# Running sums through memory, substitution in turns, and other places for weights in a three-block network kernel

## The chip, the cores and the metric

The kernel runs on one core of one Trainium2 chip. The metric is the device time of one execution in microseconds (us). The kernel before takes 1947.57 us, the median of three runs (1945.8 to 1948.2).

## The reference

The input x has 256 tokens of 1024 channels, in fp32 throughout. A first block runs two layers, each of four sublayers with an RMS norm before and after: an FFN (1024 to 2816 to 1024, SiLU-gated, half residual), a mixer, a cross attention to a memory of 256 tokens, and another FFN. A second block of one layer follows (a state-space branch beside dilated attention, then an FFN of the same sizes) and a last norm.

The mixer is where most of the change lies. It has retention heads beside four gated delta-rule heads of 128 channels, the latter in both directions over the sequence in chunks of 64. What bears on the change:

```python
g = jnp.cumsum(g.reshape(b, h, n, c), axis=-1)
decay = jnp.exp(jnp.where(tril, g[..., :, None] - g[..., None, :], -jnp.inf))
lower = jnp.where(strict, jnp.einsum('bhnid,bhnjd->bhnij', k_beta, k) * decay, 0.0)
sol = lax.linalg.triangular_solve(lower, rhs, left_side=True, lower=True, unit_diagonal=True)
```

## The kernel before

**Weight products.** Every product with a weight is three fp32r matmuls (`mm3`, L168 to L172), since a weight is kept as a high part `hi` and a rest `lo`: hi·hi, hi·lo, lo·hi. A unit of weights (128 x 1024) comes by DMA from SP's queue into a `raw` tile (L143), ACT makes `hi` from it (L148), DVE `lo` (L149). In the trace L170, L171 and L172 are therefore nearly all of PE's matmuls. There are two ways to multiply: with the activations stationary and 512 columns of weights moving ("by tokens", and DN), or with the weights stationary and 256 columns of activations moving ("by channels").

**Pools.** A pool that isn't named otherwise is opened on the left side of SBUF and stacked upward; in the map of this program `raw` (4 buffers of 4 KB a partition) ends at 42 KB, `wts` (4 `hi`, 4 `lo`) lies at 42 to 75 KB, `xT` at 73 to 108 KB with what follows it, and `hT` of the FFNs (the hidden activations as `hh` and `hl`) at 125 to 154 KB. The pool `w2` (8 `hi`, 8 `lo`), opened on the right side by `more_weights`, lies at 160 to 229 KB.

**Order.** A list scheduler fixes the order on each engine: it takes instructions by their order in the program, but when the next one of an engine isn't ready it takes a later one that is. So PE is filled with later matmuls wherever their inputs stand ready. `issue_after` puts an instruction behind another one.

**An FFN** (L312) goes over 11 slices j of 256 hidden channels. Slices 0 and 1 are made by tokens, since the input's second half comes late (`by_tokens`, with the Tanh of L364, DVE's L365 and L366, and PE's transposes of L371); 2 to 10 by channels (`by_channels`, twice 48 matmuls each). DN(t, j) (L408) multiplies slice j with its rows of the down weights for token half t: 12 matmuls of 512 columns, four products of three. `wpool` (L329) says from which pool a unit's `hi` and `lo` come: for slice 1, and for the down weights of slices 0 and 7 to 10, `w2`; for slice 10's gate and up `wts`; of the others every third call gets `wts`, which is one of the four gate/up units and the first of the two down units of a slice. After the loop the program's order is DN(0,8), DN(0,9), DN(0,10), fin(0), DN(1,7) to DN(1,10), and fin(1), put off to the next stage. `fin(t)` is the norm chain of token half t: squares of the two accumulators on ACT (L205), the inverse root on POOL (L189 to L213), the residual on DVE (L298, L300), and the next norm the same way again, until DVE writes `xg` (L237) and PE transposes it (L250).

With `defer`, the next stage's first norm factor is applied later: `set_pre` (L254) writes xg (L235) without the factor and then queues the squares for the factor. In `ffn` the second half's `fin` runs as `run_late` behind by_tokens(0, 0) in the program (L436 to L438).

**The mixer** (L724). `strengths` (L752) is a generator whose steps are hung into the stream of projections at q steps, by the dictionaries at L958. Its third step makes the sums `ngl` (L764), its fourth and fifth call `decays(0)` and `decays(1)` (L795). For a direction, `decays` makes the running sum of g at all partitions: per token half, four fp32 matmuls with one column of g, repeated over 128 columns, stationary against the triangle `tri` (L805), and a matmul that adds the mask from `identr` and `mskr` (L807). Three such groups (near, far, and the columns 256:384) go through 12 Exps on ACT (L812, L815, L818) from PSUM to E, which `pairs` and `products` (L992, L1000; PE at L1003) use.

**The substitution** `solve` (L1117) solves the chunks of 64 in both directions. Each step makes eight 64-row matmuls (as 64*64 tiles) with M (L1145) and with the diagonal inverses (L1153), over four heads and two directions; the directions lie on opposite halves of the partitions. The program emits both directions in turn, but the scheduler is free to take one direction's first.

## Time and profile before

| | |
|---|---|
| median of three runs | 1947.57 us (1945.8 to 1948.2) |
| the profiled execution | 1947.42 us |
| its span, first to last instruction | 1945.2 us |
| granted TensorE clock, mean | 0.998 of full speed |
| HBM read | 333.90 MB, 172 GB/s over the span |

The span is what the page's shares refer to; the profiled execution's own time is 2.2 us longer, for what lies around it. Times in a timeline are microseconds from the start of the span. A matmul's recorded time is longer than the step from its start to the next one's, since they are pipelined; the steps are what add up. An fp32 matmul appears as two records, an fp32r one as one.

### The profile page before, as it was taken

What the parts mean: (1) busy time and instruction counts of PE and PEld (TensorE: products, weight loads), DVE (VectorE), ACT (ScalarE), POOL (GpSimd) and SP (SyncE); (2) the same over time, 40 slices, a digit from 0 to 9 for tenths busy, and PEclk for the clock granted to TensorE, in tenths of its full rate; (3) what the DMA queues carried; (4) which work ended last, traced back from release to release, by engine and by line L of the source; (5) the groups of instructions that cost most, each with busy time, mean ns of one, the idle gap of its engine ahead of it and who ended that gap; (6) DMA issues with size and microseconds to landing.
All of it is one profiled execution on the core that took longest, in us unless ns stands there. A gap on an engine that the chain in (4) does not pass through costs nothing.

```text
span 1945.2 us, 34675 instructions
## 1 busy us (share of the span) xinstructions
PE 1914.7 (98%) x12859; PEld 1717.7 (88%) x12859; DVE 1412.7 (73%) x3002; ACT 1048.9 (54%) x2173; POOL 185.7 (10%) x407
## 2 busy tenths in 40 slices
PE   9999999999999999999999999999999999999998
PEld 6899888898899989999788978998999998888997
DVE  6777688775666766667987757666798988767765
ACT  5655465465554555546555645554555555546542
POOL 2000100020200110010100120002101111001000
PEclk9999999999999999999999999999999999999999
DMA  8666434364566556644434726655566646656651
GB/s 266 206 220 217 125 109 147 109 220 137 164 205 196 180 186 220 187 161 144 137 101 145 247 86 212 200 189 157 146 174 182 187 121 205 200 196 224 199 179 49
DMA packets 272887, 337.26 MB, mean 173 GB/s; under 512 B 19740, under 2 KB 223150, under 8 KB 272718
## 3 DMA queue, kind: packets, MB, share of 16 engines
q1 hardware_dynamic: 266980, 326.64, 53.6%
q10 hardware_dynamic: 5690, 8.25, 1.2%
q8 instruction: 101, 1.65, 0.3%
q14 instruction: 68, 0.56, 0.1%
q0 software_dynamic: 48, 0.16, 0.0%
HBM read 333.90 MB, written 1.08 MB: 172 GB/s over the span
## 4 chain that ended last, share of the span: by engine, by line
PE 84%; DVE 4%; POOL 3%; DMA 2%; ACT 2%; issue 2%; SPq 0%; ACTq 0%; POOLq 0%; DVEq 0%
PE bank L170 25%; PE bank L171 25%; PE bank L172 25%; DVE lo L149 2%; DMA raw<-in_ffn_up_dram 2%; PE bank L250 1%; POOL t L192 1%; POOL vh L213 1%; POOL y L193 1%; ACT hi L148 1%; PE bank L1003 1%; PE bank L1543 1%; ACT md L1034 1%; PE bank L1153 1%; PE bank L1256 1%
## 5 line engine op out<-in xcount | busy, mean ns | idle before, releaser
L148 ACT ACTIVATE hi<-raw 128x512 fp32r<-128x512 f32 (+1 forms) x1190 | 678.7, 615 | 413.6 <-PE bank L172 96.0
L149 DVE TENSOR_TENSOR lo<-raw,hi 128x512 fp32r<-128x512 f32 (+1 forms) x1190 | 764.7, 680 | 187.1 <-ACT hi L148 178.4
L170 PE MATMUL bank<-xh,hi 128*128 128x256 f32 x2080 | 588.8, 283 | 0.0
L171 PE MATMUL bank<-xl,hi 128*128 128x256 f32 x2080 | 585.1, 281 | 0.0
L172 PE MATMUL bank<-xh,lo 128*128 128x256 f32 x2080 | 584.7, 281 | 0.1
L170 PEld LDWEIGHTS bank<-xh,hi 128*128 128x128 f32 x2080 | 394.2, 190 | 4.1
L171 PEld LDWEIGHTS bank<-xl,hi 128*128 128x128 f32 x2080 | 393.9, 189 | 3.5
L172 PEld LDWEIGHTS bank<-xh,lo 128*128 128x128 f32 x2080 | 394.5, 190 | 0.6 <-DVE lo L149 0.6
L170 PE MATMUL bank<-hi,xh 128*128 128x512 f32 (+1 forms) x852 | 333.5, 392 | 3.5 <-ACT xh L175 2.2
L171 PE MATMUL bank<-lo,xh 128*128 128x512 f32 (+1 forms) x852 | 324.7, 381 | 5.2 <-DVE lo L149 5.1
L172 PE MATMUL bank<-hi,xl 128*128 128x512 f32 (+1 forms) x852 | 323.9, 380 | 0.5 <-DVE xl L177 0.5
L171 PEld LDWEIGHTS bank<-lo,xh 128*128 128x128 f32 x852 | 160.3, 188 | 34.8 <-DVE lo L149 9.9
L170 PEld LDWEIGHTS bank<-hi,xh 128*128 128x128 f32 x852 | 160.2, 188 | 31.5 <-ACT xh L175 3.5
L172 PEld LDWEIGHTS bank<-hi,xl 128*128 128x128 f32 x852 | 159.9, 188 | 28.8 <-DVE xl L177 2.2
L170 PE MATMUL bank<-hi,hh 128*128 128x512 f32 x440 | 175.9, 400 | 1.3 <-ACT hh L175 1.3
L171 PE MATMUL bank<-lo,hh 128*128 128x512 f32 x440 | 173.9, 395 | 0.0
L172 PE MATMUL bank<-hi,hl 128*128 128x512 f32 x440 | 173.4, 394 | 0.0
L213 POOL TENSOR_SCALAR vh<-ss 128x1 f32<-128x1 f32 x40 | 27.6, 689 | 1130.8 <-ACT junk L205 996.1
L402 ACT ACTIVATE th<-s 128x256 f32<-128x256 f32 x90 | 37.3, 414 | 124.3 <-DVE s L401 122.7
L172 PEld LDWEIGHTS bank<-hi,hl 128*128 128x128 f32 x440 | 82.7, 188 | 20.7 <-DVE hl L177 0.3
L170 PEld LDWEIGHTS bank<-hi,hh 128*128 128x128 f32 x440 | 82.7, 188 | 18.4 <-ACT hh L175 1.7
L171 PEld LDWEIGHTS bank<-lo,hh 128*128 128x128 f32 x440 | 82.7, 188 | 16.0
(369 smaller groups left out, 1991.4 us busy)
## 6 DMA issues: line engine op xcount, KB each, us to landing
raw<-in_w_in_dram SPq DMA_DIRECT2D x112, 512.0 KB, 4.4
raw<-in_ffn_gate_dram SPq DMA_DIRECT2D x176, 256.0 KB, 3.9
raw<-in_ffn_up_dram SPq DMA_DIRECT2D x176, 256.0 KB, 4.3
raw<-in_ffn_down_dram SPq DMA_DIRECT2D x88, 512.0 KB, 4.6
raw<-in_w_in_dram SPq DMA_DIRECT2D x96, 192.0 KB, 2.8
raw<-in_w_ffn_gate_dram SPq DMA_DIRECT2D x44, 256.0 KB, 3.8
raw<-in_w_ffn_up_dram SPq DMA_DIRECT2D x44, 256.0 KB, 4.1
raw<-in_w_ffn_down_dram SPq DMA_DIRECT2D x22, 512.0 KB, 4.6
```

Of the source, the lines that this page charges most:

```text
L148: nc.scalar.activation(hi[:, c], raw[:, c], AF.Copy)
L149: nc.vector.tensor_tensor(lo[:, c], raw[:, c], hi[:, c].bitcast(F32), ALU.subtract)
L170: mm(out, lhsT=lh, rhs=rh, start=start, stop=False)
L171: mm(out, lhsT=lh, rhs=rl, start=False, stop=False)
L172: mm(out, lhsT=ll, rhs=rh, start=False, stop=stop)
L192: V.tensor_scalar(t, y, y, vh, ALU.mult, ALU.mult)
L193: V.tensor_scalar(y, t, -1.5, y, ALU.add, ALU.mult)
L213: V.tensor_scalar(vh, s[:, 0:1], s[:, 1:2], 0.5 * EPS, ALU.add, ALU.add)
L250: self.nc.tensor.transpose(b[:, i * P:(i + 1) * P], src[:, (q + i) * P:(q + i + 1) * P], self.ident)
L402: last["A"] = nc.scalar.activation(th, s[:, 0], AF.Tanh)
L1003: T.matmul(b[:, j * 256:(j + 1) * 256], lhsT=lhs[:, h, j * P:(j + 1) * P], rhs=rhs[:, h], start=True, stop=True)
L1034: A.activation(md[r, :, :, :, s], mn[r, :, :, c0:c0 + 16].rearrange("p n h a -> p a h n"), AF.Copy, scale=self.half[s][r])
```

## The change

It has four parts.

1. Decays: per layer, four matmuls with the four columns of g stationary give the running sums of both directions and token halves on four partitions; ACT copies them to SBUF, a DMA on GpSimd's queue writes them to memory, and two others read them back to all 128 partitions, 512 KB each. GpSimd adds the mask (`msk`, fp32, in place of `mskr`; `identr` goes), and the Exps read SBUF, the far group first, before the mask is added to its half. The steps of `strengths` are hung at other q.
2. `solve` chains its matmuls so that the directions alternate on PE.
3. `wpool` puts the down weights of slices 2 to 7 into `wts` and all gate and up weights but slice 10's into `w2`; the pool `raw` moves to the right side, so that what lies above it on the left comes 16 KB lower.
4. In an FFN's `run_late`, the squares of the deferred norm are put behind the Tanh of by_tokens(0, 0).

```diff
@@ -73,7 +73,7 @@
         nc = self.nc
         pool = self.pool
         self.cp = pool(ctx, "const", 1)
-        self.rawp = pool(ctx, "raw", 4)
+        self.rawp = ctx.enter_context(tc.tile_pool(name="raw", bufs=4, side="right", reuse_waits="tile"))
         self.wp = pool(ctx, "wts", 4)
         self.xp = pool(ctx, "xT", 2)
         self.nrm = pool(ctx, "nrm", 1)
@@ -98,6 +98,8 @@
 
         self.fence = []
 
+        self.behind = []
+
     def first_block(self, ctx):
 
         self.fp = self.pool(ctx, "first", 1)
@@ -105,8 +107,7 @@
         self.tri.append(self.one(C_TB, P))
         self.half = [self.one(C_HALF + i, 1) for i in range(2)]
         self.odd = [self.one(C_HALF + 2 + i, 1) for i in range(2)]
-        self.identr = self.fp.tile([P, P], F32R, name="identr")
-        self.mskr = [self.fp.tile([P, P], F32R, name=f"mskr{d}") for d in range(2)]
+        self.msk = [self.fp.tile([P, P], F32, name=f"msk{d}") for d in range(2)]
         self.lnret = self.fp.tile([P, 16], F32, name="lnret")[:, 0:1]
         self.nc.gpsimd.memset(self.lnret, -0.5 * math.log(128.0))
 
@@ -258,7 +259,10 @@
         r = None if defer else self.rstd(self.halves(self.x[t]), D, pool)
         xg = self.normed(self.x[t], g, r)
         if defer:
-            r = self.rstd(self.halves(self.x[t]), D, pool)
+            with ExitStack() as es:
+                for ins in self.behind:
+                    es.enter_context(self.tc.issue_after(ins))
+                r = self.rstd(self.halves(self.x[t]), D, pool)
             rh, r2 = self.small(1, "rh"), self.small(1, "r2")
             pool.tensor_scalar(rh, r, 0.5, None, ALU.mult)
             self.mark = pool.tensor_scalar(r2, rh, r, None, ALU.mult)
@@ -321,17 +325,15 @@
             hT = {}
             acc = {}
             pend = []
-            cnt = [0]
             last = {}
             factor = self.factor
             rows = []
 
             def wpool(kind, j):
 
-                cnt[0] += 1
-                if j == 1 or kind == "dn" and (j > 6 or j == 0):
-                    return w2
-                return self.wp if j == 10 or cnt[0] % 3 == 0 else w2
+                if kind == "dn":
+                    return self.wp if 1 < j < 8 else w2
+                return self.wp if j == 10 else w2
 
             def load_gu(j):
                 return [[u.rearrange("p (k a f) -> p k a f", k=2, a=2) for u in self.gate_up(wg, wu, j, q, wpool("gu", j))] for q in range(4)]
@@ -434,7 +436,9 @@
             xT = self.xT
             by_tokens(0, 0)
             done = [last["A"].ins, last["V"].ins]
+            self.behind = done[:1]
             self.run_late()
+            self.behind = []
             by_tokens(0, 1, {4: flush, 6: lambda: self.take_pre(1)})
             self.fence = done
 
@@ -646,9 +650,8 @@
         nc.scalar.dma_start(self.cst1, self.a["consts"][:, C_ONE:C_END])
         once = self.nrm.tile([P, C_ALL - C_END], F32, tag="xg", name="once", bufs=2)
         nc.scalar.dma_start(once, self.a["consts"][:, C_END:])
-        nc.scalar.copy(self.identr, self.ident)
         for d, c0 in enumerate((C_MF, C_MB)):
-            nc.scalar.copy(self.mskr[d], once[:, c0 - C_END:c0 - C_END + P])
+            nc.scalar.copy(self.msk[d], once[:, c0 - C_END:c0 - C_END + P])
         self.cs1 = []
         for t in range(2):
             wk = self.nrm.tile([P, 512], F32, tag="junk", name="wk")
@@ -727,6 +730,7 @@
         w_in = a["w_in"][l]
         with ExitStack() as es:
             bp = self.pool(es, "mix", 1)
+            dp = es.enter_context(self.tc.tile_pool(name="drows", bufs=1, space=bass.MemoryType.DRAM))
             wk = self.pool(es, "mixw", 6)
             ch4 = lambda: bp.tile([P, 1024], F32, tag="ch4", name="ch4", bufs=8)
             xg4 = lambda: self.nrm.tile([P, D], F32, tag="xg", name="xg4", bufs=2)
@@ -763,6 +767,17 @@
                     for d in range(2):
                         T.matmul(pg[:, t * 8 + d * 4:t * 8 + d * 4 + 4], lhsT=self.tri[d], rhs=g[:, t, d * 4:d * 4 + 4], start=True, stop=True)
                 V.tensor_scalar(ngl, pg[:, 0:16].rearrange("p (t c) -> p t c", t=2), -1.0, None, ALU.mult)
+
+                b, r = self.bank(), w512()
+                for d in range(2):
+                    for t in range(2):
+                        T.matmul(b[0:4, (2 * d + t) * P:(2 * d + t + 1) * P], lhsT=g[:, t, d * 4:d * 4 + 4], rhs=self.tri[d], start=True, stop=True)
+                A.copy(r[0:4], b[0:4])
+                rows_d = dp.tile([2, 2, 4, P], F32, name="rows_d")
+                nc.gpsimd.dma_start(rows_d.rearrange("d t h c -> h (d t) c"), r[0:4].rearrange("h (x c) -> h x c", c=P))
+                for d in range(2):
+                    rows.append(ch4())
+                    nc.gpsimd.dma_start(rows[d], rows_d[d].rearrange("t h c -> (t h c)").unsqueeze(0).to_broadcast([P, D]))
                 yield
                 decays(0)
                 yield
@@ -790,7 +805,7 @@
             def values(n, hooks={}, between=None):
                 return (self.proj_tokens(mT, a["xattn_v"][l], n * 512, put_v(n), between=between), 4, hooks)
 
-            E, ngc = [None, None], S("ngc", 8)
+            E, ngc, rows = [None, None], S("ngc", 8), []
 
             def decays(d):
                 E[d] = bp.tile([P, 4, 384], F32, tag=f"E{d}", name="E")
@@ -799,23 +814,17 @@
                 c = slice(d * 4, d * 4 + 4)
                 near, far = (slice(0, P), slice(P, 2 * P)) if d == 0 else (slice(P, 2 * P), slice(0, P))
 
-                def rows(t, masked):
-                    b = self.bank()
-                    for h in range(4):
-                        T.matmul(b[:, h * P:(h + 1) * P], lhsT=g[:, t, d * 4 + h:d * 4 + h + 1].to_broadcast([P, P]), rhs=self.tri[d], start=h == 0, stop=h == 3 and not masked)
-                    if masked:
-                        T.matmul(hd(b), lhsT=self.identr, rhs=self.mskr[d].unsqueeze(1).to_broadcast([P, 4, P]), start=False, stop=True)
-                    return hd(b)
-                b = rows(f, True)
-                V.tensor_tensor(ngc[:, c], b[:, :, end], ngl[:, f, c], ALU.add)
+                R = rows.pop(0).rearrange("p (t h c) -> p t h c", t=2, h=4)
+                mask = self.msk[d].unsqueeze(1).to_broadcast([P, 4, P])
+                V.tensor_tensor(ngc[:, c], R[:, f, :, end], ngl[:, f, c], ALU.add)
+                nc.gpsimd.tensor_tensor(R[:, f], R[:, f], mask, ALU.add)
                 for h in range(4):
-                    A.activation(E[d][:, h, near], b[:, h], AF.Exp, bias=ngl[:, f, d * 4 + h:d * 4 + h + 1])
-                b = rows(s, False)
+                    A.activation(E[d][:, h, far], R[:, s, h], AF.Exp, bias=ngc[:, d * 4 + h:d * 4 + h + 1])
+                nc.gpsimd.tensor_tensor(R[:, s], R[:, s], mask, ALU.add)
                 for h in range(4):
-                    A.activation(E[d][:, h, far], b[:, h], AF.Exp, bias=ngc[:, d * 4 + h:d * 4 + h + 1])
-                b = rows(s, True)
+                    A.activation(E[d][:, h, near], R[:, f, h], AF.Exp, bias=ngl[:, f, d * 4 + h:d * 4 + h + 1])
                 for h in range(4):
-                    A.activation(E[d][:, h, 256:384], b[:, h], AF.Exp, bias=ngl[:, s, d * 4 + h:d * 4 + h + 1])
+                    A.activation(E[d][:, h, 256:384], R[:, s, h], AF.Exp, bias=ngl[:, s, d * 4 + h:d * 4 + h + 1])
 
             def sums(x, tag):
 
@@ -955,7 +964,7 @@
             side = strengths()
             s = lambda: next(side, None)
             fill = self.stream([
-                values(0, between=lambda: self.take_pre(1)), *qkv(1, {0: s}), *qkv(2, {0: s, 1: s, 3: s}),
+                values(0, between=lambda: self.take_pre(1)), *qkv(1, {0: s, 3: s}), *qkv(2, {2: s, 3: s}),
                 tokens(512, "rk", {3: lambda: turn("rk")}),
                 tokens(1024, "rv", {2: lambda: backs["rk"](), 3: take_rv}),
                 tokens(0, "rq", {3: lambda: turn("rq")}),
@@ -1120,6 +1129,8 @@
                 halves = (slice(0, 64), slice(64, P))
                 order = (halves, halves[::-1])
                 Z = [inv[d].rearrange("p (h n) i -> p h n i", h=4) for d in range(2)]
+                turns = [(h, d) for h in range(4) for d in range(2)]
+                in_turn = lambda one: self.tc.issue_after(one.ins) if one else nullcontext()
                 for n in range(2):
                     y = [hd(Y[d][:, seq[d][n]]) for d in range(2)]
                     rhs = [hd(R[:, seq[d][n]]) for d in range(2)]
@@ -1139,18 +1150,20 @@
                         if m:
 
                             bs = [self.bank() for _ in range(2)]
-                            for h in range(4):
-                                for d in range(2):
-                                    o = order[d][0]
-                                    T.matmul(bs[d][r[d], h * P:(h + 1) * P], lhsT=M[d][o, h, cols[d] + r[d].start:cols[d] + r[d].stop], rhs=y[d][o, h], start=True, stop=True)
+                            one = None
+                            for h, d in turns:
+                                o = order[d][0]
+                                with in_turn(one):
+                                    one = T.matmul(bs[d][r[d], h * P:(h + 1) * P], lhsT=M[d][o, h, cols[d] + r[d].start:cols[d] + r[d].stop], rhs=y[d][o, h], start=True, stop=True)
                             for d in range(2):
                                 V.tensor_tensor(y[d][r[d]], hd(bs[d])[r[d]], rhs[d][r[d]], ALU.add)
                                 rhs[d] = y[d]
                             yield
                         bs = [self.bank() for _ in range(2)]
-                        for h in range(4):
-                            for d in range(2):
-                                T.matmul(bs[d][r[d], h * P:(h + 1) * P], lhsT=Z[d][r[d], h, n], rhs=rhs[d][r[d], h], start=True, stop=True)
+                        one = None
+                        for h, d in turns:
+                            with in_turn(one):
+                                one = T.matmul(bs[d][r[d], h * P:(h + 1) * P], lhsT=Z[d][r[d], h, n], rhs=rhs[d][r[d], h], start=True, stop=True)
                         A.copy(y[0][r[0]], hd(bs[0])[r[0]])
                         V.tensor_copy(y[1][r[1]], hd(bs[1])[r[1]])
                         yield
```

## Rows read from the trace of the kernel before

**Rows 1.** the page's first part: busy time and share of each engine.

```profile
PE 1914.7 (98%) x12859; PEld 1717.7 (88%) x12859; DVE 1412.7 (73%) x3002; ACT 1048.9 (54%) x2173; POOL 185.7 (10%) x407
```

**Rows 2.** the waits of PE: total us, times, longest us.

```profile
PE bank L371 <- DVE h L366: 4.7, 3, 1.7
...
PE bank L250 <- DVE xg L237: 2.7, 3, 1.3
```

**Rows 3.** PE's timeline, the first decays and E's first use: start, us, line, operation.

```profile
238.40 1.05 PE L805 MATMUL bank<-cst,g 128*128 128x128 f32 x8
...
239.21 0.47 PE L807 MATMUL bank<-mskr,identr 128*128 128x512 f32 x1
...
241.53 0.28 PE L170 MATMUL bank<-xh,hi 128*128 128x256 f32 x1
...
260.45 1.89 PE L1003 MATMUL bank<-ch 128*128 128x256 f32 x8
```

**Rows 4.** a window of the first mixer: PE, PEld, DVE, ACT, POOL busy, clock, DMA.

```profile
262.00:266.00 4.00, 4.00 (x19) 3.35 (x18) 4.00 (x20) 0.85 (x2) 0.00 (x0) 1.00 0.44 131
```

**Rows 5.** lines L213, L1526, L812 (ns min/median/max); POOL and DVE timelines at 673.

```profile
L213 POOL TENSOR_SCALAR vh<-ss x40: 286/301/4797, 5.6 to 1750.5; 128x1 f32<-128x1 f32 x40
...
673.95 4.80 POOL L213 TENSOR_SCALAR vh<-ss 128x1 f32<-128x1 f32 x1 [2.83 <-ACT junk L205]
...
673.68 4.90 DVE L149 TENSOR_TENSOR lo<-raw,hi 128x512 fp32r<-128x512 f32 x8
...
L1526 POOL TENSOR_TENSOR w<-xs,dsk x8: 1042/1288/1360, 1403.1 to 1608.9; 128x512 f32<-128x512 f32 x8
...
L812 ACT ACTIVATE E<-bank,ngl x16: 360/369/388, 240.6 to 916.3; 128x128 f32<-128x128 f32 x16
```

**Rows 6.** DMA issues: count, KB each, median us to landing.

```profile
rows<-rows_d SPq DMA_DIRECT2D x8, 512.0 KB, 4.9
...
rows_d<-w SPq DMA_DIRECT2D x1, 32.0 KB, 1.5
```

**Rows 7.** PE's timeline, substitution: both directions, then one alone.

```profile
332.38 1.09 PE L1153 MATMUL bank<-ch,iv 64*64 64x128 f32 x16
...
338.69 1.08 PE L1145 MATMUL bank<-ch,M 64*64 64x128 f32 x8
```

**Rows 8.** PE's timeline: first and last starts of runs of weight products.

```profile
104.09 0.28 PE L170 MATMUL bank<-xh,hi 128*128 128x256 f32 x1
...
109.76 0.40 PE L170 MATMUL bank<-hi,hh 128*128 128x512 f32 x1
...
173.75 0.28 PE L171 MATMUL bank<-xl,hi 128*128 128x256 f32 x1
...
185.15 0.39 PE L170 MATMUL bank<-hi,hh 128*128 128x512 f32 x1
...
204.74 0.39 PE L170 MATMUL bank<-hi,xh 128*128 128x512 f32 x1
...
250.42 0.39 PE L170 MATMUL bank<-hi,xh 128*128 128x512 f32 x1
...
255.65 0.39 PE L172 MATMUL bank<-hi,xl 128*128 128x512 f32 x1
```

**Rows 9.** timelines at FFN ends: ACT and DVE 186:205, PE at the second block.

```profile
192.34 0.60 ACT L205 ACTIVATE junk<-bank 128x512 f32<-128x512 f32 x1 [3.48 <-PE bank L172]
...
203.08 1.42 DVE L237 SCALAR_TENSOR_TENSOR xg<-x,y,gain 128x512 f32<-128x512 f32 x2 [4.04 <-POOL y L193]
...
1359.08 1.10 PE L250 MATMUL bank<-cst,xg 128*128 128x128 f32 x6 [1.31 <-DVE xg L237]
```

**Rows 10.** timelines of ACT and DVE at the start of an FFN.

```profile
496.79 0.45 ACT L364 ACTIVATE th<-bank,rh 128x256 f32<-128x256 f32 x1
...
495.89 1.29 DVE L235 TENSOR_TENSOR xg<-x,gain 128x512 f32<-128x512 f32 x2
...
497.28 0.42 DVE L365 SCALAR_TENSOR_TENSOR th<-th,bank 128x256 f32<-128x256 f32 x1
```

More of the change, by code (lines that the diff above doesn't have):

```diff
@@ L1 @@
 import math
-from contextlib import ExitStack
+from contextlib import ExitStack, nullcontext
 import numpy as np
```

## The prediction

> **What bounds the kernel.** The profile page comes first: PE is busy 1914.7 us, 98% of the span of 1945.2, no other engine over 73% [rows 1]. The waits of PE come second: no cause reaches 6 us, and the two that this change can touch make 4.7 and 2.7 us [rows 2]. So the time is the length of PE's stream of matmuls, and a change is worth what it takes out of that stream or what new holes it opens in it. Third is the timeline of PE around each edit, where start-to-start steps are read, not durations: matmuls overlap, and a 512-column one recorded with 0.39 us starts only about 0.23 us after its forerunner [rows 8]. Last, the other engines' windows in the mixer: DVE is full there in stretches (4.00 of 4 us from 262 to 266 [rows 4], the same in the window before it and from 282 to 302), so what PE gains in the mixer need not all reach the end.
>
> The profiled execution took 1947.42 us (span 1945.2), the median is 1947.57; the sum is made against 1947.4. A measurement tells some 0.2% (3.9 us) from no change.
>
> **Part 1, running sums by way of memory.** One decays call holds PE from 238.40 to 241.53, 3.13 us [rows 3]; it runs for two directions and two layers: 4 × 3.13 = 12.5 us leave PE. Added per layer: four two-pass matmuls of 128 columns, as the four at 238.40 to 239.21, 0.81 us [rows 3], so 1.8 us for two layers with the change of tile. PE: −10.7 us.
> What else is added per layer: an ACT copy of 4x512 (under 0.6 us on an engine that has room before 258 us), a 32 KB write and two 512 KB broadcast reads on POOL's queue, and four 128x512 POOL adds. The nearest rows: such a read landed after 4.9 us from SP's queue [rows 6], such an add took 1.04 to 1.36 us [rows 5]. The new matmuls stand where the strengths step makes its sums now, one q, some 4 us, ahead of 238.40 [rows 3]; from there 2 us for matmuls and copy (estimate), write 1.5, read 4.9 [rows 6], two adds 2.6, twelve Exps 4.4 (12 × 369 ns [rows 5]): the first direction is complete near 250, the second near 253, while the first use of E comes after the products at 260.45 [rows 3]. That leaves 7 us, so the path itself should cost nothing. The Exps stay as many; the PSUM banks that they held are freed.
> Not all 10.7 us arrive. After 258 us DVE is full for stretch upon stretch [rows 4]; and POOL and DVE hold each other up: at 673.95 a 128x1 POOL instruction that takes 301 ns by the median of its line lasted 4.80 us, the time of a DVE row of eight subtractions, 673.68 to 678.58 [rows 5]. Four adds of 1.3 us per layer can so take up to 5 us from DVE. Bounds: −10.7 and 0. I take about half, −5.7: DVE has slack before 258 us and none behind.
> The Trainium skill, "SBUF — State Buffer", section "🔬 SBUF: two separate sides", speaks against this part: a DVE instruction with two SBUF inputs and a GpSimd one that reads SBUF exclude each other for their whole length, and a GpSimd-queue DMA can starve for descriptors while DVE holds the port. By it the adds would cost DVE the full 5 us a layer and the gain would be near nothing. The long POOL row agrees with the first half; no run here shows the second.
> The reordered Exps and the copies of the mask cost nothing: the same count, under other work.
>
> **Part 2, substitution in turns.** A group of both directions together (x16) lasts 1.09 us; one direction alone (x8) lasts 1.08 us [rows 7]. So two directions in turn are as cheap as one: 64-row tiles of opposite halves run side by side. Three of six groups per layer stand split in the trace (338.69 and its partner at 342.20; 344.27 and 345.71; 354.60 and 356.04), six in all; pairing each saves up to 1.08 us on PE. The first matmul may go alone where one direction's input is later. Take −5.5, bounds −2 and −7. What waits for the later direction has other matmuls as filler.
>
> **Part 3, where weights and activations lie.** PE's step depends on where its operands lie. By the program's map the raw pool ends at 42 KB of a partition, wts lies at 42 to 75, xT at 73 to 108, hT at 125 to 154, w2 at 160 to 229. Out of wts with xh (both low) 23 steps of 512 columns take 250.42 to 255.65, 227 ns each; in the tail, out of w2 with hh (both high), 84 take 185.15 to 204.74, 233 ns [rows 8]. A kernel-wide mean over such steps would lie nearer 228.4 and 233.5 (estimate), 5 ns apart. Channel products go the other way, with weights stationary: slice j=10, all out of wts, takes 120.0 ns (95 steps, 173.75 to 185.15), a slice with three of four units in w2 118.1 ns (48, 104.09 to 109.76), so w2 alone 117.5 [rows 8].
> The change puts gate and up of j=2 to 9 wholly into w2: one unit in four, 8 × 24 × 5 FFNs = 960 steps × 2.5 ns = −2.4 us. It puts down slices 2 to 7 (6 × 24 × 5 = 720 steps, now half or wholly from w2) into wts, and with raw moved away hT sinks by 16 KB into the low part: 720 × 4.9 ns = −3.5 us; only −1.6 if hT does not matter. One unit of j=0 goes high: 60 steps × 6 ns, +0.4. Sum −5.0 with a discount, bounds −2.5 and −6.
>
> **Part 4, the tail of an FFN.** Slice 7 of down now sits in wts, of four buffers, which slice 10 of gate and up needs whole. Its last two units can be converted only when DN(1,7) is done, which stood behind fin(0). So DN(0,8), DN(0,9), DN(1,7) and perhaps DN(1,8) go ahead of the second half of by_channels(0,10). PE loses nothing there, but fin(0)'s chain (squares at 192.34, xg to 203.08 + 1.42 = 204.50: 12.2 us [rows 9]) was covered by four DNs, 48 × 0.233 = 11.2 us; one to two and a half (2.8 to 6.8 us) remain, I take two, so 5.6 us of cover go. At the two mixer ends the memory's values fill (0.6 each); at the deferred end, whose chain is shorter, 1.1; at the second block, where PE already waits at 1359.08 [rows 9], 3.5 with less left to wait for later; at the very end 0.5. Sum +6, bounds 0 and +12.
>
> **Part 5, squares behind the first Tanh.** The Tanh starts at 496.79, when the squares are through; but DVE's L365, which needs it, also stands behind L235 (495.89 + 1.29 = 497.18), starts at 497.28 [rows 10]; PE's longest such wait is 1.7 us [rows 2]. An earlier Tanh gains 0.1 us; if DVE's order turned too, 1.5. Four places: −0.3, bounds 0 and −5.
>
> **Sum:** −5.7 − 5.5 − 5.0 + 6 − 0.3 = −10.5; 1947.4 − 10.5 = **1937 us**.
>
> **Rivals.** (a) **Slower: the tail decides.** If only DN(0,10)'s successor DN(1,10) is left behind fin(0), 8.4 us of cover are missing, and the two chains of t=0 and t=1 meet on POOL, where each norm takes some 3 us. Priced 8.4 at the second block, 6 at the deferred end, 3 at each mixer end, 1.5 last: +22. With parts 2, 3 and 5 and no gain in part 1: 1947.4 − 10.8 + 22 = 1958; with half of part 1, 1953. It decides once the cover falls below some 4 us. For: the four buffers; against: the memory's values run 10 us past the FFN's end. Chance 0.11.
> (b) **Decays turn into a wait**: the reads or adds held up by DVE make E late by some 5 to 8 us a layer, past the slack of 7 with DVE's saturation behind it; part 1 goes from −5.7 to between 0 and +10: 1943 to 1953, likeliest 1947, no change. For: the 4.80 us row; against: DVE has pauses before 258 us. Chance 0.17.
> (c) **Everything arrives**: the tail covered, all of part 1: 1947.4 − 10.7 − 5.5 − 5.0 − 0.3 = 1926. For: PE is the bound nearly everywhere; against: DVE's full windows. Chance 0.2.
> (d) **Places don't matter**: the steps differ for another reason, PSUM or order, and part 3 gives nothing: 1942. Chance 0.07. The forecast (1931 to 1943) has the rest, 0.45.
>
> **Numbers.** Faster by over 0.2% (under 1943.5): the forecast, (c), most of (d) and a little of (b), 0.72. Within: most of (b), the edge of the others, 0.15. Slower: (a) and the end of (b), 0.13. A tenth outside on each side: 1926 to 1948.
>
> **What would show it.** L805 and L807 are gone and the new four stand once per layer; L1145 and L1153 come only as x16 rows of about 1 us; DN slices 2 to 7 step at 228 ns, channel slices 2 to 9 at 117.5; DN(1,7) stands before the end of by_channels(0,10), and L250's wait for xg grows; L371's wait stays. It is wrong if PE waits for E or DVE's long waits fill the mixer, if steps don't follow the place, or if xg waits grow by over 15 us.

## The result and the profile after

The changed kernel takes 1964.98 us (median of 4 runs, 1962.8 to 1969.5) against 1947.88 (1945.8 to 1949.6) in the same rounds: ratio 1.0091, 95% interval 1.0078 to 1.0104. It is slower by 17 us, where a gain of 10.5 us was forecast (1931 to 1943 us). The profiled execution took 1963.98 us, span 1962.2. All times of runs are of undisturbed executions; one of e8's eight, of 7250.06 us, is left out.

The page's first part, of the kernel after [rows 1]:

```profile
PE 1911.8 (97%) x12771; PEld 1709.4 (87%) x12771; DVE 1422.3 (72%) x3002; ACT 1053.0 (54%) x2174; POOL 202.9 (10%) x421
```

PE has 88 instructions less, yet is busy only 2.9 us less, and idles for 50.4 us of the span instead of 30.5. The waits of PE after, then those of before that are not in [rows 2]; line numbers differ by one or two between the kernels:

```profile
PE bank L172 <- DVE lo L150: 9.2, 10, 2.6
PE bank L171 <- ACT hi L149: 6.0, 7, 1.6
PE bank L251 <- DVE xg L238: 4.7, 3, 3.3
PE bank L373 <- DVE h L368: 4.4, 3, 1.5
PE bank L171 <- DVE M L1007: 3.6, 2, 3.2
PE bank L171 <- ACT hh L176: 3.4, 1, 3.4
```

```profile
PE bank L171 <- DVE lo L149: 5.1, 7, 1.2
...
PE bank L170 <- ACT hh L175: 1.3, 1, 1.3
PE bank L170 <- ACT hi L148: 1.2, 2, 0.9
```

All but the wait at L373 (L371 before) have grown, and the one for M is new. Only L1007's M (3.6 us, 3.2 of it in the second mixer) is made from E; the rest are waits for weights' parts (hi, lo), for norms (xg), for activations (hh). The clock is the second thing to see. Windows of PE after, and one of before; columns busy time, granted clock, DMA share, GB/s:

```profile
104.00:110.00 6.00, 5.49 (x27) 0.72 0.96 316
184.00:192.00 8.00, 7.04 (x37) 0.57 0.45 153
274.00:280.00 6.00, 4.26 (x15) 0.72 0.27 87
944.00:950.00 6.00, 4.64 (x15) 0.72 0.00 1
1374.00:1380.00 6.00, 4.39 (x20) 0.72 0.13 48
```

```profile
184.00:192.00 8.00, 8.00 (x41) 1.00 0.88 264
```

In five places of the changed kernel a hole of PE (a stretch in which it stands idle) is followed by a stretch at half clock (1.2 GHz), of 3.4 us in four and 6.9 in one. Before, the clock fell only in the last microseconds. (1 - clock) times the length of each window gives up to 4 x 1.7 + 3.4 = 10.2 us lost.

Where the 17 us arose, by the time at which PE reaches the same column of its weight products (after minus before):

```
stretch (time before, us)                  change, us
100-110     first FFN, hh late, 1.2 GHz      +5.2
172-205     first FFN's end, 1.2 GHz         +5.7
222-320     first mixer, decays              +3.4
332-362     its substitution                 -1.9
542-651     one steady FFN                   -0.9
651-676     that FFN's end                   +1.0
770-880     FFN and its end                  +2.6
890-985     second mixer, decays             +2.7
1000-1030   its substitution                 -1.9
1355-1372   entry of the second block        +3.2
all others                                   -2.1
```

**The mixers.** Windows of the same two stretches of work, before and after; columns as in [rows 4]:

```profile
222.00:320.00 98.00, 95.90 (x827) 84.86 (x826) 84.79 (x250) 61.28 (x132) 5.68 (x8) 1.00 0.49 150
890.00:985.00 95.00, 92.63 (x803) 81.70 (x801) 82.95 (x244) 60.18 (x130) 5.66 (x8) 1.00 0.49 148
```

```profile
230.67:332.11 101.44, 93.62 (x783) 80.70 (x782) 87.98 (x250) 62.92 (x133) 12.89 (x15) 0.98 0.50 155
902.80:1000.52 97.72, 90.15 (x758) 77.02 (x757) 86.38 (x244) 61.73 (x131) 13.40 (x15) 0.98 0.50 155
```

PE's idle time goes from 98.00 - 95.90 = 2.1 to 7.8 us, and from 2.4 to 7.6. Its busy time falls by 2.3 and 2.5 only, though 10.7 / 2 = 5.35 us of matmuls a layer should be gone by the forecast. So 3.1 and 2.9 us of busy time have come in: -5.35 + 5.7 + 3.1 = +3.4, and -5.35 + 5.2 + 2.9 = +2.7. One stretch at 1.2 GHz in each layer (274, 944) accounts for 1.7 us of that; what the rest is stays open. The path itself, timelines of PE, ACT, POOL and DVE after [rows 3]; this stretch lies 8.7 us later than before (230.67 - 222):

```profile
243.03 1.04 PE L774 MATMUL bank<-cst,g 128*4 128x128 f32 x8
...
251.58 0.56 ACT L775 COPY w<-bank 4x512 f32<-4x512 f32 x1
...
252.45 0.64 POOL L777 DMA_DIRECT2D rows_d<-w  x1 [29.51 <-ACT w L775]
256.43 1.08 POOL L780 DMA_DIRECT2D ch<-rows_d  x2 [3.34 <-DMA rows_d<-w]
...
261.91 0.16 DVE L819 TENSOR_TENSOR ngc<-ch,ngl 128x4 f32<-128x4 f32 x1 [3.48 <-DMA ch<-rows_d]
...
272.34 0.68 ACT L827 ACTIVATE E<-ch,ngl 128x128 f32<-128x128 f32 x2
272.92 3.22 ACT L149 ACTIVATE hi<-raw 128x512 fp32r<-128x512 f32 x6
...
276.07 0.50 PE L172 MATMUL bank<-lo,xh 128*128 128x512 f32 x1 [1.74 <-DVE lo L150]
```

The matmuls start where the forecast had them (243.03 - 8.7 = 234.3). Then the copy stands 7.5 us in ACT's queue, the write takes 4.0 to the reads' issue, the read 5.5, and Exps and adds 11: E is complete for both directions at 273.0, in before's time 264.3, not 253, and so behind the products at 260.45 [rows 3] that its first use follows. Two queues pay: DVE stands still 3.48 us at ngc with conversions of weights behind it, and ACT then works off twelve Exps a direction before six conversions in a row at 272.92. PE waits for the low parts at 276.07 and, for 2.59 us, at 291.28. DMA issues after [rows 6]:

```profile
ch<-rows_d POOLq DMA_DIRECT2D x4, 512.0 KB, 6.0
...
rows_d<-w POOLq DMA_DIRECT2D x2, 8.0 KB, 3.5
rows_d<-w SPq DMA_DIRECT2D x1, 32.0 KB, 3.0
```

**The first FFN and its end** [rows 8, 9]. Timelines of ACT and PE after:

```profile
101.16 0.63 ACT L149 ACTIVATE hi<-raw 128x512 fp32r<-128x512 f32 x1 [1.80 <-DMA raw<-in_ffn_up_dram]
104.05 0.42 ACT L176 ACTIVATE hh<-th 128x256 fp32r<-128x256 f32 x1 [1.43 <-DVE th L406]
104.52 0.50 PE L171 MATMUL bank<-hi,hh 128*128 128x512 f32 x1 [3.38 <-ACT hh L176]
...
179.00 1.15 ACT L149 ACTIVATE hi<-raw 128x512 fp32r<-128x512 f32 x2 [2.57 <-DMA raw<-in_ffn_down_dram]
...
183.42 0.39 PE L171 MATMUL bank<-xh,hi 128*128 128x256 f32 x1 [1.59 <-ACT hi L149]
...
185.24 0.58 PE L173 MATMUL bank<-xh,lo 128*128 128x256 f32 x1 [0.96 <-DVE lo L150]
...
188.21 1.15 ACT L149 ACTIVATE hi<-raw 128x512 fp32r<-128x512 f32 x2 [4.32 <-PE bank L172]
```

At 101 ACT stands at a conversion whose weights have not landed, with the Tanh that makes hh behind it. At 183 slice 10 has two of the four wts buffers, since slice 7 of down holds the others until after fin(0). In the middle of the slice PE waits for the next unit's conversion (1.59 us for hi, 0.96 for lo), and the conversion at 188.21 stands 4.32 us until PE has let a buffer go; PE, at 1.2 GHz by then, does not wait for that one. Ahead of the first wait ACT had also stood 2.57 us for weights of down that landed late, so the two buffers need not be all of it.

**Substitution and steps** [rows 7, 8]. A group of the substitution that stood split before, and a steady FFN (12 products of down from the first row to the second); after, then before:

```profile
350.80 0.43 PE L1157 MATMUL bank<-ch,M 64*64 64x128 f32 x2
353.92 1.08 PE L1157 MATMUL bank<-ch,M 64*64 64x128 f32 x14
...
603.38 0.40 PE L171 MATMUL bank<-hi,hh 128*128 128x512 f32 x1
606.13 0.28 PE L171 MATMUL bank<-xh,hi 128*128 128x256 f32 x1
```

```profile
593.47 0.40 PE L170 MATMUL bank<-hi,hh 128*128 128x512 f32 x1
596.27 0.28 PE L170 MATMUL bank<-xh,hi 128*128 128x256 f32 x1
```

The groups are paired but for their first matmul, which gains 1.9 us a layer. A step of the down weights' products fell from 2.80 / 12 = 233 to 2.75 / 12 = 229 ns.

### The profile page after: what moved, and what is told of

The parts are those of the page before. It is cut to its first block, busy times and chain, and to the rows that moved or that the text cites. A ratio compares the mean times of both kernels' runs of the same rounds, so it can differ in the third digit from the quotient of the medians.

```text
span 1962.2 us, 34520 instructions
## 1 busy us (share of the span) xinstructions
PE 1911.8 (97%) x12771; PEld 1709.4 (87%) x12771; DVE 1422.3 (72%) x3002; ACT 1053.0 (54%) x2174; POOL 202.9 (10%) x421
## 4 chain that ended last, share of the span: by engine, by line
PE 73%; DVE 8%; DMA 6%; issue 5%; POOL 4%; ACT 4%; SPq 0%; ACTq 0%; POOLq 0%; DVEq 0%
PE bank L171 22%; PE bank L173 21%; PE bank L172 21%; DVE lo L150 3%; DMA raw<-in_ffn_up_dram 2%; ACT hi L149 2%; DMA raw<-in_ffn_down_dram 1%; POOL t L193 1%; PE bank L251 1%; POOL vh L214 1%; POOL y L194 1%; DMA raw<-in_xattn_o_dram 1%; ACT md L1043 1%; PE bank L1556 1%; DMA ch<-rows_d 1%
## 5 line engine op out<-in xcount | busy, mean ns | idle before, releaser
L403 DVE TENSOR_TENSOR s<-bank,rows 128x512 f32<-128x512 f32 x90 | 61.8, 686 | 77.1 <-PE bank L173 45.8
```

Source lines behind the costliest of these rows:

```text
L403: nc.vector.tensor_tensor(s, bb, rows[0], ALU.mult)
```

## The experiments

Theory: part 1 costs by queues that stand waiting for the read; the places cost by buffers now shared at an FFN's end; both are dearer by the clock. Rivals: the port lock of POOL and DVE, descriptors of POOL's queue, the moved hooks, the copy in ACT's queue, a place that is worse. Parts are numbered as in the prediction: its part 4 is what the new places cost at an FFN's end, and its part 5 is the fourth part of the change. Code is shown cut. Each ratio is against the kernel before in the same rounds, with its 95% interval.

**The parts alone.** e1_sums: the decays' edits (first_block, strengths, decays, hooks) only.

> The kernel before with part 1 alone (sums through memory). My theory from the two traces: PE loses 10.7 us of matmuls, but E now hangs on a path of ACT copy, write (3.5 us to land), read (6.0 us) and adds, and DVE's ngc waits in DVE's queue for the read; in the changed kernel the two mixers came out some 3 us slower each in this stretch. Expected: 4 to 8 us slower than before. Rival, port lock between POOL and DVE: about as slow, but then with DVE and POOL instructions stretched and no wait for the DMA. Rival, this part is free and gains: 8 to 11 us faster, and all the loss lies in the other parts.

e2_turns: the substitution's `in_turn` only.

> The kernel before with part 2 alone (substitution in turns). My theory: faster by some 3.8 us (the changed kernel gained 1.9 us in each substitution), that is 1.0 us for each of four paired groups. By the prediction: faster by 5.5 us, all six pairs. Rival, pairs add waits for the later direction: no change.

e3_places: rawp on the right and the new wpool only; e4_places7 the same with

```diff
-                    return self.wp if 1 < j < 8 else w2
+                    return self.wp if 1 < j < 7 else w2
```

> The kernel before with part 3 alone (down slices 2 to 7 in wts, gate and up in w2, raw on the right). My theory: the places of the operands gain some 4.5 us over the five FFNs, and slice 10 of gate and up, which finds only two of its four buffers free, costs 1 to 6 us at each FFN's end, with a fallen clock behind the wait; a weight that lands late in the first FFN and a late xg at the second block cost 2 to 3 us each. Sum: 6 to 12 us slower. Rival, these waits come from part 1's changed timing: then this part alone is 4 to 5 us faster.

> Part 3 alone, but the down weights of slice 7 in w2 as before, so that slice 10 of gate and up has four buffers. If the two occupied buffers are the cause: the waits at the ends go and the kernel is 3 to 5 us faster than before. If the raw pool's move or w2's fuller use is the cause: as slow as with part 3 whole.

Measured: e1 1957.18 us, ratio 1.0043 (1.0030 to 1.0057); e2 1941.92, 0.9974 (0.9963 to 0.9985); e3 1957.53, 1.0046 (1.0033 to 1.0058); e4 1951.20, 1.0022 (1.0009 to 1.0034). By the ratios part 1 alone costs 8 us and the places 9; only the turns gain, 5.1. In sum that is 12 us (14 by the medians) against 17 of the whole; each of the four has an interval of 2.1 to 2.6 us to either side, so whether the parts cost more together stays open. Slice 7 in w2 gives back some 5 us by the ratios (6.3 by the medians), and the holes at the FFN's end go; another opens, where a norm's squares come late (e4's timeline of PE):

```profile
173.95 1.29 PE L250 MATMUL bank<-cst,xg 128*128 128x128 f32 x8 [1.97 <-DVE xg L237]
```

The waits of e1, DVE's and PE's:

```profile
DVE ngc L814 <- DMA ch<-rows_d: 7.4, 3, 4.0
...
PE bank L170 <- DVE lo L148: 9.2, 10, 2.5
```

**What in part 1?** Each of these is e1 with one edit. e5_sums_late: the decays two hooks later. e6_sums_dveadd: mask adds by DVE. e10_sums_hooks: hooks as before. e11_sums_actq: write and reads from ACT's queue. e14_sums_copydve: the copy by DVE. In this order, one line each of those that change alike:

```diff
-                values(0, between=lambda: self.take_pre(1)), *qkv(1, {0: s, 3: s}), *qkv(2, {2: s, 3: s}),
-                tokens(512, "rk", {3: lambda: turn("rk")}),
+                values(0, between=lambda: self.take_pre(1)), *qkv(1, {0: s, 3: s}), *qkv(2),
+                tokens(512, "rk", {0: s, 2: s, 3: lambda: turn("rk")}),
...
-                nc.gpsimd.tensor_tensor(R[:, f], R[:, f], mask, ALU.add)
+                V.tensor_tensor(R[:, f], R[:, f], mask, ALU.add)
...
-                values(0, between=lambda: self.take_pre(1)), *qkv(1, {0: s, 3: s}), *qkv(2, {2: s, 3: s}),
+                values(0, between=lambda: self.take_pre(1)), *qkv(1, {0: s}), *qkv(2, {0: s, 1: s, 3: s}),
...
-                nc.gpsimd.dma_start(rows[d], rows_d[d].rearrange("t h c -> (t h c)").unsqueeze(0).to_broadcast([P, D]))
+                nc.scalar.dma_start(rows[d], rows_d[d].rearrange("t h c -> (t h c)").unsqueeze(0).to_broadcast([P, D]))
...
-                A.copy(r[0:4], b[0:4])
+                V.tensor_copy(r[0:4], b[0:4])
```

> Part 1 alone, with decays(0) and decays(1) called two q later in the stream (the sums are written and read where part 1 does it). My theory, DVE standing still before ngc until the read has landed (7.4 us in three waits in the run of part 1 alone): those waits go, and the kernel is 3 to 8 us faster than with part 1 alone, near the kernel before or below. Rival, E comes too late for the products: then later calls make it worse, by some 3 us or more. Rival, port lock by the adds: no change against part 1 alone.

> Part 1 alone, with the four mask adds on DVE instead of GpSimd. If the lock between POOL and DVE is the cause: 3 us or more faster than part 1 alone. By my theory (the landing of the read, not the adds): within 3 us of part 1 alone, the waits of ngc for the DMA as long as there (7 us).

> Part 1 alone with the strengths' steps hung where the kernel before has them (sums a q later, decays a q earlier or at the same). If the moved steps matter (PE waiting 1.6 us for g, the clock falling in two runs behind it): 2 to 4 us faster than part 1 alone. If the reading back is what counts: as slow or slower, since the read then starts later against the first use of E, with ngc's waits longer than 7 us in sum.

> Part 1 alone, the write and the two reads issued from ACT's queue instead of GpSimd's. If descriptors made by GpSimd under DVE's lock delay them: landing falls from 6.0 us to 4 or less, the write from 3.5 to some 1.5, and the kernel is 3 us or more faster than part 1 alone. If the memory path is slow whoever issues it: landing 5 us or more and at most 2 us gained.

> Part 1 alone, the four-partition copy by DVE instead of ACT, where it stood 7.5 us behind the matmuls in ACT's queue (233.8 to 241.3). If the lateness of the path counts: the write goes out some 5 us earlier, the wait of ngc for the read falls from 7.4 to under 3 us and the kernel is 2 to 5 us faster than part 1 alone. Rival, DVE's queue delays it as much: no change.

Measured: e5 1953.87, 1.0034 (1.0021 to 1.0047); e6 1953.38, 1.0028 (1.0017 to 1.0039); e10 1957.79, 1.0059 (1.0045 to 1.0072); e11 1951.61, 1.0030 (1.0020 to 1.0040); e14 1953.75, 1.0035 (1.0023 to 1.0047). None reaches the kernel before, none can be told from e1 (the intervals overlap), and DVE's wait at ngc is 8.3, 7.4, 7.6, 7.5 and 5.2 us in them. The lock is worth 0.15% at the most likely, e6 against e1, and perhaps nothing. Descriptors of POOL are not it either, as e11's DMA issues and wait show:

```profile
ch<-rows_d ACTq DMA_DIRECT2D x4, 512.0 KB, 6.4
```

```profile
DVE ngc L814 <- DMA ch<-rows_d: 7.5, 3, 3.5
```

The Trainium skill, "SBUF — State Buffer", section "🔬 SBUF: two separate sides", says that DVE, in an operation that takes the port it shares with POOL, can hold up a DMA of POOL's queue by starving it of descriptors, and not one of ACT's queue. Here the read landed in 6.4 us from ACT's queue and in 6.2 from POOL's (e1): the page's case is not this one.

**Nobody waits for the read?** e9_sums_ngc: ngc's totals from two small matmuls instead of from the rows.

```diff
+                for d in range(2):
+                    T.matmul(pg[:, 16 + 4 * d:20 + 4 * d], lhsT=self.ones.to_broadcast([P, P]), rhs=g[:, d, d * 4:d * 4 + 4], start=True, stop=True)
...
-                V.tensor_tensor(ngc[:, c], R[:, f, :, end], ngl[:, f, c], ALU.add)
```

> Part 1 alone, but ngc's totals come from two small matmuls with ones instead of from the rows read back, so that DVE waits for no DMA. By the theory that DVE's standing still before ngc (7.4 us in three waits, weights' low parts queued behind it) costs most: those waits go, the holes of PE before low parts shrink, 3 to 6 us faster than part 1 alone, that is 0 to +4 against the kernel before. Rival, the late E itself holds PE up, whoever waits: within 2 us of part 1 alone, ACT's Exps waiting instead. Rival, hooks: the wait of 1.6 us for g and what follows is the main part: no gain.

e13_sums_early and e16_sums_early2: the rows come from an input, read at the start of the strengths or one step later, and the Exps have a constant bias, so that the running sums are left out of E. e17_sums_ahead: a scaled constant goes through memory ahead of the sums, with the same bias.

```diff
+                    nc.gpsimd.dma_start(rows[d], a["norm_pre"][l, d].unsqueeze(0).to_broadcast([P, D]))
...
-                    A.activation(E[d][:, h, far], R[:, s, h], AF.Exp, bias=ngc[:, d * 4 + h:d * 4 + h + 1])
+                    A.activation(E[d][:, h, far], R[:, s, h], AF.Exp, bias=self.lnret)
```

> Part 1 alone, but the rows that the Exps use are read at the first step of the strengths from a row of an input, without the write, and the Exps' biases are a constant: the running sums themselves are left out of E, while the matmuls, the copy, the two reads, the adds, the Exps and their order stay. If the length of the path through memory (copy to landing 10 us and more, E late) is why part 1 doesn't pay: no wait of DVE for the read, fewer holes and no fallen clock in the mixer, 5 us or more faster than part 1 alone, up to 8 us faster than the kernel before. If the added engine work or the moved steps are the cause: as slow as part 1 alone.

> As the run with the rows read early (the running sums left out of E, constant biases, no write), but the reads one step of the strengths later, so that the Exps don't mix into the norm at the mixer's entry, where the last run opened holes of 2.2 and 5.0 us. If the path through memory is what part 1 loses by: the entry as in the kernel before, 4 us gained in each mixer, 4 to 8 us faster than the kernel before (1939 to 1943 us). If the mixer can't use PE's 10.7 us anyhow: 1947 or more.

> Part 1 alone, but what goes through memory is a scaled constant that is there some 8 us before the sums (right behind the strengths' be), and the Exps' biases are a constant: the running sums are left out of E; matmuls, copy, write, reads, adds and Exps all stay. The path through memory so ends about 15 us earlier, and nothing of it can run at the mixer's entry. In the mixer itself (from 222 to 320 us of the kernel before, and the same stretch of the second layer) part 1 alone lost 3.0 and 3.2 us, the two runs with early reads gained 2 to 2.5. If the path's length is what part 1 loses by: 2 to 4 us gained in each mixer, no hole at the entry, 1941 to 1945 us. If the mixer can't use PE's 10.7 us anyhow: 1947 or more.

Measured: e9 1953.09, 1.0034 (1.0021 to 1.0046); e13 1953.79, 1.0038 (1.0026 to 1.0050); e16 1953.35, 1.0027 (1.0016 to 1.0038); e17 1953.65, 1.0044 (1.0030 to 1.0058). In e9 DVE no longer waits, but ACT takes its place; in e17 the Exps wait too, and behind them the sums. Waits of e9, then of e17:

```profile
ACT E L820 <- DMA ch<-rows_d: 9.5, 2, 5.4
```

```profile
ACT E L819 <- DMA ch<-rows_d: 7.5, 2, 3.8
...
PE bank L770 <- DVE g L765: 5.2, 2, 4.9
```

None can be told from e1, where the theory had a gain of 3 us or more in each. In e13 and e16 the mixers gain 2.2 and 2.5, 1.7 and 2.5 us by PE's progress (stretches 222 to 320 and 890 to 985 of before), about half of 5.35 each. But the reads and Exps ran ahead into the mixer's entry, and its norm came late: PE lost 2.2 and 6.7, 2.2 and 6.3 us there (205 to 222, 880 to 890), so that part of the loss may only have moved. e16, meant to cure this, was a miss. Timeline of PE, e13:

```profile
886.58 1.97 PE L249 MATMUL bank<-cst,xg 128*128 128x128 f32 x8 [4.86 <-DVE xg L236]
```

**Places again.** e7_raw: rawp on the right alone (with it hT goes low). e8_turns_behind_raw: this, the turns and part 5. e12_turns_wpool7: the turns and e4's wpool, rawp left. e15_after_dn7: the whole change with e4's wpool.

```diff
-        self.rawp = pool(ctx, "raw", 4)
+        self.rawp = ctx.enter_context(tc.tile_pool(name="raw", bufs=4, side="right", reuse_waits="tile"))
```

> The kernel before with the raw pool alone on the right side: no order changes, only addresses, 16 KB lower on the left. If the place of the hidden activations matters as part 3 of the prediction has it (2.9 ns on each step whose weights lie low): the 300 steps of down units in wts gain 0.9 us and a few others as much again: 1 to 2 us faster, no new waits. Rival, places don't matter: no change.

> Parts 2 and 4 and the raw pool's move together, without the sums through memory and without the new sharing of wts and w2. Expected: part 2's 4 to 5 us, 1 to 2 of the move, 0.3 of the Tanh: 5 to 7 us faster than before, 1941 to 1942 us, the fastest so far. Rival, the parts disturb each other as in the changed kernel: slower than part 2 alone.

> Substitution in turns and part 3's sharing of wts and w2 with slice 7 of down in w2, the raw pool left where it was. By the rates read in the traces: 4 to 5 us from the turns and some 4 us from the places, 1939 us, if no hole opens; with the holes of the run with slice 7 in w2 (memory norm's xg, 2.1 us twice, and a fallen clock behind them) 1945 to 1947. This tells whether the gain of the places can be had.

> The whole change, but slice 7 of down in w2. By the difference of the runs with part 3 (5 to 6 us): 1959 us. If parts 1 and 2 move the stages so that the memory norm's hole doesn't open: down to 1955. If the FFN's end isn't what slice 7 spoils in the whole change: 1965.

Measured: e7 1948.36, 1.0006 (0.9998 to 1.0015); e8 1942.26, 0.9974 (0.9963 to 0.9984); e12 1944.44, 0.9991 (0.9981 to 1.0001); e15 1960.49, 1.0071 (1.0059 to 1.0083). hT's place gives nothing: twelve products of down in e7, from the first row to the second, take 2.80 us as before.

```profile
594.72 0.40 PE L170 MATMUL bank<-hi,hh 128*128 128x512 f32 x1
...
597.52 0.28 PE L170 MATMUL bank<-xh,hi 128*128 128x256 f32 x1
```

Part 5 gives nothing that can be told apart. The places do not pay even beside the turns: e12 is at 0.9991 where the turns alone are at 0.9974. Slice 7 in w2 takes some 4 us off the whole change (ratios 1.0091 and 1.0071), as it did some 5 off e3.

**The clock.** Two holes of e4 have the same cause and nearly the same length: the one at 173.95 above, 1.97 us, and one of 2.01 us in the next layer. PE was full for 16 us ahead of each. The second in PE's timeline, and the windows of PE behind the first and the second:

```profile
845.11 1.71 PE L250 MATMUL bank<-cst,xg 128*128 128x128 f32 x8 [2.01 <-DVE xg L237]
```

```profile
176.00:178.00 2.00, 2.00 (x19) 1.00 0.69 221
...
846.00:848.00 2.00, 2.00 (x11) 0.50 0.65 199
```

After the one the clock stays at 2.4 GHz, after the other it falls to 1.2: 19 instructions in 2 us against 11. The runs of e4 lie between 1944.95 and 1957.75 us, and the mean granted clock of the fastest is 0.999, of the slowest 0.995: 0.004 of 1950 us is about 8 of the 13 us between them.

The fastest is e2, the turns alone: 1941.92 us, faster than both kernels; e8 can't be told from it.

## Why the prediction was wrong

**Part 1 (-5.7 forecast, +8.4 measured alone; the largest error).** Which matmuls leave PE was right. The step that failed is "the path itself should cost nothing", with E complete near 250 and 253. As a chain of durations the path was put at 16 to 19 us; it took 30, since the copy stood 7.5 us in ACT's queue, the write took 4.0 instead of 1.5, and Exps and adds 11. The write is of 8 KB, not 32, and the 32 KB row of SP's queue in [rows 6] was no measure for it: that row itself took 3.0 us in the changed kernel. So the slack of 7 us was used up, and PE waited 3.2 us for M in the second mixer. Worse, the slack was counted for E's use and not for the instructions queued behind ngc and the Exps: DVE and ACT work in order, and weights' conversions stood behind them. That these queues are what costs most is read from the waits and not shown: e9 took DVE's wait away, and its time can't be told from e1's. Rival (b) had the term, 0 to +10, and named DVE's saturation; but not the wait at ngc, and it had 0.17. The lock that the discount to a half was for is small or nothing (e6). How much of the 10.7 us a path would keep that nobody waits for stays open: e13, e16 and e17 each opened a hole elsewhere. One rival no run touches: the rows that are read back hold two of the mixer's eight ch4 buffers.

**Part 2 (-5.5 forecast, -5.1 measured, -3.8 of it in PE's progress).** Right within the interval; that the first matmul may go alone was said too.

**Part 3 (-5.0 forecast).** Right in size where the work is steady: 0.8 to 1.1 us an FFN, about -4.5. The place of the weights matters, moving ones (233 to 229 ns a step) more than stationary ones; hT's does not (e7). So rival (d) is out. What the part left out is that units moved between pools land and come free at other times: holes near 104 come with it (e3, e4), and one at 174 with slice 7 in w2 (e4). That the changed order of buffers makes those weights late is argued, not shown.

**Part 4 (+6 forecast).** The place was right, slice 7's buffers, and the mechanism wrong: DN(1,7) was not hoisted; it still stood behind fin(0). Slice 10 ran on two buffers instead, and PE waited in the middle of it, 5.7 us at the first FFN's end with the clock. e3 against e4 sizes it at some 5 us, the whole change against e15 at some 4, either to about 3 us. Parts 3 and 4 together were forecast at +1 us and came to +9 alone (e3).

**Part 5 (-0.3 forecast).** As forecast: not to be told from nothing.

**The clock** was in no term of the forecast: up to 10.2 of the 17 us. The wait for L371 stays, as forecast, and xg waits grew by 2.0, far under the 15 named as proof against it.

## What to carry to other kernels

Where PE is full, work taken off it is worth what its replacement leaves untouched: for every new transfer, list the instruction that waits for it and everything behind that one on its engine, since an in-order queue passes the wait on to work that has nothing to do with it. Buffers that are shared anew have to be counted where two slices need them at once, by the unit, before any gain of place. A hole in a full matmul stream can cost twice, once as idle time and once as slow matmuls after it; which holes do so could not be told here from their length.

## What the runs showed of the hardware

- Holes of PE in a stream that was dense otherwise, of 2.0 us (e4) and 3.4 us (the changed kernel, at 104), were followed by 3.4 us at 1.2 GHz; holes of the same cause and nearly the same length went either way (1.97 and 2.01 us, e4). The Trainium skill, "TensorE: Matmul & The Clock Gate", section "HAM oscillation — how this bites in real kernels", tells of waits on transfers after which TensorE starts slow again; the windows here agree (0.72 from 104 to 110, behind 3.38 us of wait), and show it for waits on DVE and ACT too.
- A 512 KB broadcast read landed 6.0 us after its issue from POOL's queue and 6.4 from ACT's (medians). An 8 KB write from POOL's queue took 3.5 us in the changed kernel and 1.9 in e14, and one 32 KB write from SP's queue 1.5 us before and 3.0 after: a single row is a poor measure of a landing.
- A 512-column product of the down weights stepped in 233 ns with half or all of its moving weights in w2, high in a partition, and in 229 with them in wts, low; moving hh 16 KB lower changed nothing (2.80 us for twelve in e7 as before).
